# Two rotary tables move to the other queue's ring, behind the first slab, and an 8 KB transfer is put in front

## The chip, the cores and the metric

The kernel runs on one core of a Trainium2 chip. The metric is device time of one execution in microseconds (us), the median of three runs for the kernel before. Smaller is better.

## The reference

A rotary embedding: each head's two halves are rotated by tables that depend on the position alone. `x` is 16 x 512 x 1024 in float32, 16 heads of 64, so `half_dim` is 32; `cos` and `sin` are 512 x 32.

```python
x = x.reshape(batch, seq, num_heads, head_dim)
x1, x2 = x[..., :half_dim], x[..., half_dim:]
cos = cos[None, :, None, :]
sin = sin[None, :, None, :]
rotated = np.concatenate([x1 * cos - x2 * sin,
                          x1 * sin + x2 * cos], axis=-1)
```

## The kernel before, in words

The input is cut into 8 slabs of two batches, 4 MB each. A slab stands in SBUF as 128 partitions x 8192 float32: a partition has 8 consecutive rows of 1024, so one DMA of a slab is 128 descriptors of 32 KB. There are 6 slab buffers. A slab is worked on in place and stored from the same buffer.

Two queues issue DMAs. SyncE issues all loads of slabs (`load`, line 61): slabs 0 to 5 at the start, slabs 6 and 7 when the stores of slabs 0 and 1 have freed their buffers. ScalarE issues all stores (line 147), between its own casts, and in the kernel before also the two tables (`load_tables`, line 77). Each issuing engine feeds a ring of its own; the same 16 DMA engines serve both rings.

The tables take a way of their own. `cos` and `sin` are read as 16 rows of 4 KB each (`TR = 16`) into every eighth partition of the tile `raw`, which VectorE has set to zero before (line 69); the first table DMA waits for that memset. GpSimd builds 0/1 and -1 selection matrices in `pick` (lines 89 and 93), waits for both tables and casts `raw` to bf16 (`raw_b`, line 99). Then 16 matmuls (line 104) spread the 16 rows over the 128 partitions, and VectorE copies the result from PSUM into `tab` (line 110), the table that every later multiply reads. So no multiply can start before the tables have landed.

After that the slabs go through a pipeline of passes, half a slab each for the first and the last two slabs, a whole one for the others. ScalarE casts a pass to bf16 (line 129), one pass ahead; VectorE multiplies twice by `tab` (line 139) and adds (line 142); ScalarE casts back to float32 (line 145) and, with the last pass of a slab, issues its store.

The order of issue is written out by hand; each engine runs its instructions in program order, and the framework puts in the semaphores.

Of the kernel before, what the change touches and what calls it, by code (L numbers as in the profile page):

```python
# [2 lines left out]

# [4 lines left out]


@with_exitstack  # L10
def kernel(
    ctx: ExitStack,
    tc: tile.TileContext,
    x: bass.AP,
    cos: bass.AP,
    sin: bass.AP,
    num_heads: int,
    out: bass.AP,
):
    nc = tc.nc  # L20
    P = nc.NUM_PARTITIONS

    batch, seq, dim = x.shape
    nh = num_heads
    hd = dim // nh
    half = hd // 2
    bf16 = mybir.dt.bfloat16
    f32 = mybir.dt.float32

    nb = 2  # L30
    slots = 6
    nslabs = batch // nb
    rpp = nb * seq // P
    W = rpp * dim
    SP = seq // rpp
    TW = rpp * half

    out_flat = out.rearrange("b s h d -> b s (h d)")

    singles = ctx.enter_context(tc.tile_pool(name="singles", bufs=1))  # L40
    slabs = ctx.enter_context(tc.tile_pool(name="slabs", bufs=slots))
    psum = ctx.enter_context(tc.tile_pool(
        name="psum", bufs=1, space=bass.MemoryType.PSUM))


    def dram(t, s, a=0, n=W):
        return bass.AP(tensor=t.tensor, offset=t.offset + s * nb * seq * dim + a,
                       ap=[[W, P], [1, n]])


    def view(t, offset, *dims):
        return dataclasses.replace(t, offset=t.offset + offset,
                                   ap=[t.ap[0], *[list(d) for d in dims]])


    slab = {}


    def load(s):
        slab[s] = slabs.tile([P, W], f32, tag="slab", name="slab")  # L60
        nc.sync.dma_start(out=slab[s], in_=dram(x, s))  # L61

    TR = 16
    TQ = seq // TR // rpp
    TC = seq * half // TR
    raw = singles.tile([P, TC], f32, tag="raw")
    nc.vector.memset(raw, 0.0)  # L69


    def load_tables(queue):
        for i, src in enumerate((cos, sin)):
            to = dataclasses.replace(
                raw, offset=raw.offset + 4 * i * raw.ap[0][0],
                ap=[[P // TR * raw.ap[0][0], TR], [1, TC]])
            queue.dma_start(out=to, in_=bass.AP(  # L77
                tensor=src.tensor, offset=src.offset, ap=[[TC, TR], [1, TC]]))


    load(0)
    load_tables(nc.scalar)
    for s in range(1, slots):
        load(s)

    pick = singles.tile([P, 3 * TQ * P], bf16, tag="pick")
    nc.gpsimd.memset(pick, 0.0)  # L89
    for g in range(3):  # L90
        for j in range(TQ):
            part = view(pick, (g * TQ + j) * P + j, (SP, P // SP), (TQ, TR))
            nc.gpsimd.affine_select(  # L93
                out=part, in_=part, compare_op=mybir.AluOpType.not_equal,
                fill=-1.0 if g == 2 else 1.0, base=-4 if g else 0,
                pattern=[[0, P // SP], [-(P // TR), TR]], channel_multiplier=1)

    raw_b = singles.tile([P, TC], bf16, tag="raw_b")
    nc.gpsimd.tensor_copy(out=raw_b, in_=raw)  # L99

    acc = psum.tile([P, 2 * rpp * hd], f32, tag="acc")
    for g, at in ((0, 0), (0, half), (1, rpp * hd), (2, rpp * hd + half)):
        for j in range(TQ):
            nc.tensor.matmul(  # L104
                view(acc, at, (hd, rpp), (1, half)),
                view(pick, (g * TQ + j) * P, (1, P)),
                view(raw_b, j * TW, (half, rpp), (1, half)),
                start=j == 0, stop=j == TQ - 1)
    tab = singles.tile([P, 2 * rpp * hd], bf16, tag="tab")
    nc.vector.tensor_copy(out=tab, in_=acc)  # L110

    passes = []
    for s in range(nslabs):
        n = rpp if 1 <= s < nslabs - 2 else rpp // 2
        passes += [(s, r, n) for r in range(0, rpp, n)]


    def halves(u):
        s, r, n = u
        t = slab[s].bitcast(bf16)
        return [view(t, (2 * r + i * n) * dim, (1, n * dim)) for i in range(2)]


    def cast(u):
        s, r, n = u
        nc.scalar.copy(out=halves(u)[0], in_=view(slab[s], r * dim, (1, n * dim)))  # L129


    cast(passes[0])
    for i, u in enumerate(passes):
        s, r, n = u
        if i + 1 < len(passes):
            cast(passes[i + 1])
        lo, up = halves(u)
        for t, a in ((up, 0), (lo, rpp * hd)):
            nc.vector.tensor_mul(  # L139
                out=t, in0=lo,  # L140
                in1=view(tab, a + r * hd, (hd, n), (0, nh), (1, hd)))
        nc.vector.tensor_add(  # L142
            out=up, in0=up, in1=view(lo, half, (hd, n * nh), (-half, 2), (1, half)))

        nc.scalar.copy(out=view(slab[s], r * dim, (1, n * dim)), in_=up)  # L145
        if r + n == rpp:
            nc.scalar.dma_start(out=dram(out_flat, s), in_=slab[s])
            if s + slots < nslabs:
                load(s + slots)


# [1 line left out]
_INS = ['x', 'cos', 'sin', 'num_heads']  # L153
_OUTS = [((16, 512, 16, 64), 'float32')]

_NUMBERS = {'num_heads': 16}


# [26 lines left out]
```

## Time and profile before

| | |
|---|---|
| Median of 3 runs | 162.03 us (161.91 to 162.1) |
| The profiled execution | 161.88 us, its span 160.1 us |
| Busy: VectorE, ScalarE | 109.3 us (68%), 113.3 us (71%) |
| Busy: GpSimd, TensorE | 4.7 us (3%), 3.6 us (2%) |
| Bytes read and written | 33.69 MB and 33.55 MB, 420 GB/s over the span |
| The two DMA queues kept the 16 engines busy for | 49.3% and 48.8% of the span |
| Tables: issue to landing | `cos` 8.0 us, `sin` 10.1 us |

The profile is of one execution; its span runs from the first instruction to the last, and 1.78 us of the execution lie around it. A row of the timeline gives start and length in us, then engine, line and operation; in brackets stands how long the engine was idle before and what released it. The DMA share of a window is the mean busy share of the 16 DMA engines, with a packet counted where it starts, so that in short windows it can be over 1.

### The profile page before, as it was taken

Reading aid. Unit: us, or ns where it says so; the run is one execution under the profiler, and the core shown is the slowest. Engines: PE = TensorE matmul, PEld = TensorE weight load, DVE = VectorE, ACT = ScalarE, POOL = GpSimd, SP = SyncE. Lnnn points to the kernel's source line nnn. Section 1 sums busy time; section 2 is a strip of 40 time slices with the busy share of each in tenths; the row PEclk is TensorE's granted clock in tenths of the full one; section 3 lists DMA queues with packets and bytes.
Section 4 is the critical chain, followed back from the end, with each engine's and each line's share of the span. In section 5 each row is a group of like instructions: output and inputs, shape, how many; then the busy total and the mean of one; then the engine's idle time right before and its main releaser. Section 6 shows DMA issues by size and latency. Waiting matters only on the chain.

```text
span 160.1 us, 200 instructions
## 1 busy us (share of the span) xinstructions
PE 3.6 (2%) x16; PEld 2.3 (1%) x16; DVE 109.3 (68%) x35; ACT 113.3 (71%) x23; POOL 4.7 (3%) x18
## 2 busy tenths in 40 slices
PE   0005300000000000000000000000000000000000
PEld 0003100000000000000000000000000000000000
DVE  2000699999999989998996299939569499910000
ACT  2105939999979999999909995199995999280000
POOL 8002000000000000000000000000000000000000
DMA  7999999999999999999999999999999999999994
GB/s 246 426 385 418 393 442 475 393 418 483 409 393 483 434 393 442 475 393 409 499 401 393 508 409 393 483 434 393 434 483 393 393 516 401 393 508 409 393 475 180
DMA packets 2368, 67.24 MB, mean 420 GB/s; under 512 B 288, under 2 KB 288, under 8 KB 320
## 3 DMA queue, kind: packets, MB, share of 16 engines
q1 hardware_dynamic: 1152, 33.55, 49.3%
q10 hardware_dynamic: 1216, 33.69, 48.8%
HBM read 33.69 MB, written 33.55 MB: 420 GB/s over the span
## 4 chain that ended last, share of the span: by engine, by line
DMA 50%; DVE 21%; ACT 8%; issue 7%; PE 2%; POOLq 1%; ACTq 0%; DVEq 0%; SPq 0%
DMA slab<-in_x_dram 26%; DMA out_dram<-slab 17%; DVE slab L139 14%; DMA raw<-in_sin_dram 6%; DVE slab L142 6%; ACT slab L145 5%; ACT slab L129 3%; PE acc L104 2%; DVE tab L110 1%; POOLq L180 1%; DVE raw L69 1%; ACTq L77 0%; POOLq L99 0%; DVEq L139 0%; SPq L61 0%
## 5 line engine op out<-in xcount | busy, mean ns | idle before, releaser
L139 DVE TENSOR_TENSOR slab<-slab,tab 128x4096 bf16<-128x4096 bf16 (+1 forms) x22 | 71.6, 3260 | 14.3 <-ACT slab L129 13.8
L129 ACT CAST slab<-slab 128x4096 bf16<-128x4096 f32 (+1 forms) x11 | 56.6, 5153 | 23.1 <-DMA slab<-in_x_dram 23.1
L145 ACT CAST slab<-slab 128x4096 f32<-128x4096 bf16 (+1 forms) x11 | 56.6, 5153 | 4.6 <-DVE slab L142 4.6
L142 DVE TENSOR_TENSOR slab<-slab 128x4096 bf16<-128x4096 bf16 (+1 forms) x11 | 35.9, 3260 | 0.3
L110 DVE CAST tab<-acc 128x1024 bf16<-128x1024 f32 x1 | 1.2, 1225 | 15.5 <-PE acc L104 15.5
L104 PE MATMUL acc<-raw_b,pick 128*128 128x256 bf16 x16 | 3.6, 415 | 13.9 <-POOL raw_b L99 13.9
L129 ACT ACT_TABLE_LOAD x1 | 1.3, 1283 | 3.2 <-issue 3.2
L104 PEld LDWEIGHTS <-pick 128*128 128x128 bf16 x16 | 2.3, 142 | 14.7 <-issue 11.3
L93 POOL TENSOR_SCALAR_AFFINE_SELECT pick<-pick 128x32 bf16<-128x32 bf16 x12 | 2.1, 257 | 0.1
L69 DVE MEMSET raw<- 128x1024 f32 x1 | 0.9, 912 | 1.0 <-PEq L166 1.0
L89 POOL MEMSET pick<- 128x1536 bf16 x1 | 1.4, 1377 | 0.3 <-POOLq L166 0.3
L99 POOL CAST raw_b<-raw 128x1024 bf16<-128x1024 f32 x1 | 1.0, 1036 | 8.5 <-DMA raw<-in_sin_dram 8.5
L166 POOL MEMSET const-float32-0.0<- 128x1 f32 x1 | 0.1, 98 | 0.2 <-issue 0.2
L166 POOL MEMSET const-bfloat16-1.0<- 128x1 bf16 x1 | 0.1, 102 | 0.0
L166 POOL MEMSET const-uint8-127<- 128x1 uint8 x1 | 0.1, 102 | 0.0
L166 POOL MEMSET const-float32-1.0<- 128x1 f32 x1 | 0.1, 98 | 0.0
## 6 DMA issues: line engine op xcount, KB each, us to landing
slab<-in_x_dram SPq DMA_DIRECT2D x8, 4096.0 KB, 42.4
out_dram<-slab ACTq DMA_DIRECT2D x8, 4096.0 KB, 26.1
raw<-in_cos_dram ACTq DMA_DIRECT2D x1, 64.0 KB, 8.0
raw<-in_sin_dram ACTq DMA_DIRECT2D x1, 64.0 KB, 10.1
```

The lines of the kernel that those rows point to most:

```text
L69: nc.vector.memset(raw, 0.0)
L89: nc.gpsimd.memset(pick, 0.0)
L93: nc.gpsimd.affine_select(out=part, in_=part, compare_op=mybir.AluOpType.not_equal, fill=-1.0 if g == 2 else 1.0, base=-4 if g else 0, pat ...
L99: nc.gpsimd.tensor_copy(out=raw_b, in_=raw)
L104: nc.tensor.matmul(view(acc, at, (hd, rpp), (1, half)), view(pick, (g * TQ + j) * P, (1, P)), view(raw_b, j * TW, (half, rpp), (1, half)), ...
L110: nc.vector.tensor_copy(out=tab, in_=acc)
L129: nc.scalar.copy(out=halves(u)[0], in_=view(slab[s], r * dim, (1, n * dim)))
L139: nc.vector.tensor_mul(out=t, in0=lo, in1=view(tab, a + r * hd, (hd, n), (0, nh), (1, hd)))
L142: nc.vector.tensor_add(out=up, in0=up, in1=view(lo, half, (hd, n * nh), (-half, 2), (1, half)))
L145: nc.scalar.copy(out=view(slab[s], r * dim, (1, n * dim)), in_=up)
L166: nc = _bacc.Bacc("TRN2", target_bir_lowering=False, num_devices=1)
L180: with _tile.TileContext(nc) as tc:
```

## The change

The tables' two DMAs are issued by SyncE, after slab 0 and before slab 1. ScalarE issues a new DMA as its first instruction: 16 rows of 128 floats of `cos`, 16 descriptors of 512 B, into a tile `first` that nothing reads. It waits for nothing.

```diff
+    first = singles.tile([TR, P], f32, tag="first")
+    nc.scalar.dma_start(out=first, in_=bass.AP(
+        tensor=cos.tensor, offset=cos.offset, ap=[[TC, TR], [1, P]]))
     load(0)
-    load_tables(nc.scalar)
+    load_tables(nc.sync)
     for s in range(1, slots):
         load(s)
```

All lines behind it have numbers higher by four in the kernel after.

## The prediction

> **What bounds the kernel now.** I read the page first: the 40 slices of the span, then the DMA totals and the chain that ended last.
>
> ```profile
> DVE  2000699999999989998996299939569499910000
> ACT  2105939999979999999909995199995999280000
> DMA  7999999999999999999999999999999999999994
> HBM read 33.69 MB, written 33.55 MB: 420 GB/s over the span
> DMA 50%; DVE 21%; ACT 8%; issue 7%; PE 2%; POOLq 1%; ACTq 0%; DVEq 0%; SPq 0%
> ```
>
> The DMA row is 9 from the second slice to the next to last; VectorE and ScalarE have holes and are idle in the last 16 us. The transfers bound the kernel. Only three things can then move the end: when the byte stream starts, how many bytes it has, and how much engine time a byte takes. The next view is the timeline around the start.
>
> ```profile
> 1.96 0.56 ACTq L77 DMA_DIRECT2D raw<-in_cos_dram  x1
> 2.55 0.61 ACTq L77 DMA_DIRECT2D raw<-in_sin_dram  x1
> 12.77 1.04 POOL L99 CAST raw_b<-raw 128x1024 bf16<-128x1024 f32 x1 [8.52 <-DMA raw<-in_sin_dram]
> 13.86 7.11 ACT L129 CAST slab<-slab 128x4096 bf16<-128x4096 f32 x2 [9.38 <-DMA slab<-in_x_dram]
> 17.47 1.23 DVE L110 CAST tab<-acc 128x1024 bf16<-128x1024 f32 x1 [15.54 <-PE acc L104]
> 18.79 6.82 DVE L139 TENSOR_TENSOR slab<-slab,tab 128x4096 bf16<-128x4096 bf16 x3
> 23.57 7.02 ACT L129 CAST slab<-slab 128x8192 bf16<-128x8192 f32 x1 [2.60 <-DMA slab<-in_x_dram]
> ```
>
> The casts released by arriving slabs date the arrivals: slab 0 at 13.86, slab 1 at 23.57. A slab of 4096 KB alone in the queues takes 9.71 us, 432 GB/s. The last store is issued at 144.27 and lands 14.8 us later (the shortest landing of line 147), at 159.07. From 13.86 to there are 145.2 us for 15 more slabs' worth of loads and stores, and 15 x 9.71 is 145.7: behind slab 0 the stream has no gap. So the change is decided in the first 13.86 us. How dear the bytes are there is in the windows (core 0: window, its length, busy time of PE, PEld, DVE, ACT, POOL with counts, clock, DMA share, GB/s; a packet counts where it starts):
>
> ```profile
> 1.50:3.00 1.50, 0.00 (x0) 0.10 (x1) 0.43 (x1) 0.00 (x0) 1.43 (x6) 1.00 1.26 350
> 3.00:5.50 2.50, 0.00 (x0) 0.00 (x0) 0.00 (x0) 1.28 (x1) 1.25 (x8) 1.00 0.98 419
> 5.50:7.80 2.30, 0.00 (x0) 0.00 (x0) 0.00 (x0) 0.00 (x0) 0.00 (x0) 1.00 1.10 442
> 7.80:10.90 3.10, 0.00 (x0) 0.00 (x0) 0.00 (x0) 0.00 (x0) 0.00 (x0) 1.00 0.98 381
> 10.90:13.00 2.10, 0.00 (x0) 0.00 (x0) 0.00 (x0) 0.00 (x0) 0.23 (x1) 1.00 0.73 312
> 37.00:61.00 24.00, 0.00 (x0) 0.00 (x0) 23.14 (x6) 22.89 (x5) 0.00 (x0) 1.00 1.01 437
> ```
>
> Share divided by GB/s is engine time for a byte. The clean rate is 1.01/437, and 10.90 to 13.00 is near it. Between 5.50 and 10.90, when the tables' packets pass, it is dearer. At the clean rate 442 GB/s would be a share of 1.02, so 0.08 x 2.3 = 0.18 us is lost; 381 would be 0.88, so 0.10 x 3.1 = 0.31 us. Together 0.49 us for each engine, on top of the tables' own 128 KB (0.30 us at 432 GB/s). I call this the mixing surcharge. The first wave, 1.50 to 3.00, is one 32 KB packet for each of 16 engines (350 GB/s x 1.5 us / 16): 1.26 x 1.5 = 1.89 us instead of 1.01 x 32.8 KB x 16 / 437 GB/s = 1.21 us. So 0.68 us is lost to the cold start.
>
> **The change, part by part.**
>
> *Tables leave ScalarE's ring.* The same two DMAs, 32 descriptors of 4 KB, now stand behind slab 0 in one ring; their 0.30 us of bytes stay. What becomes of the 0.49 us? In before the small items (two table packets and two completion writes on each engine) came from a second ring between slab 0's 32 KB packets. The trace has no 4 KB packet behind a 32 KB one in the same ring, so I bound it: at the dear end nothing is saved, at the other all 0.49. The nearest row is a completion write inside SyncE's ring, at the seam of slabs 0 and 1: the window 13.00 to 23.00 has a share of 1.06 at 455 GB/s, 1.052 at the clean rate, a loss of some 0.08 us over 10 us that holds a seam. I take 0.43 us saved, nearer to that row, because the loss is not seen where one ring works alone.
>
> The Trainium skill speaks against this step ("DMA: Bandwidth & Descriptors", section "Issuing engines are not separate DMA queues"): DMAs from any issuing engine end on the same 16 DMA engines and interleave, and issuing from another one only saves issue time. By that rule alone the surcharge would follow the tables into the other ring, and this step would be worth 0 instead of 0.43 us. The page gives no price for small packets of one ring between large ones of another; the windows above do.
>
> *SyncE's queue.* The table DMAs wait for the memset of `raw` (0.91 us from 1.01, done at 1.92). They stand now in front of the issues of slabs 1 to 5. Slab 1's issue, until now right behind slab 0's, goes to about 1.96 + 0.56 + 0.61 = 3.1 us, and slabs 2 to 4 follow at some 0.4 us each (line 61 issues: median 395 ns), by 5 us. In the program's order slab 4's issue also waits for the semaphore that the short DMA uses, slab 5's still for slab 0's. All is covered by slab 0 and the tables, which keep the engines busy until about 13 us; without that cover it would cost 2 us. On ScalarE the table DMAs and their wait go; its table load can start earlier, off the path, because its first cast waits for slab 0.
>
> *The tables' landing.* Slab 0 lands earlier by 0.30 + 0.43, at 13.1. The tables come right after, at about 13.4 instead of 12.62, when sin landed. The chain behind them keeps its lengths: POOL's cast 1.04, 16 matmuls 3.57, VectorE's cast 1.23. So VectorE's first multiply moves from 18.79 to about 19.6. What is late next? ScalarE and VectorE are 0.8 us later until ScalarE meets its wait for slab 5 at 84 us, where it now idles 3.85 us (the same timeline): the delay ends there. Store 0 is later by as much, but loads fill the engines meanwhile (loads 4 and 5 are still in the ring, load 5 until 84 us). At the end, 159.07 - 9.71 = 149.4 is when the engines reach the last store, 5.1 us after its issue; an issue takes 1.0 us to the first packet (0.73 to 1.7), so some 4 us of cover remain. Cost: 0. It costs only what exceeds 3.9 us.
>
> *The short DMA.* 8 KB is 0.02 us at 432 GB/s. Each engine has two more small items from ScalarE's ring, a 512 B packet and a completion write. The trace has no such packet ahead of the stream. Upper bound: the four small items of before cost 0.49, so two cost 0.25. Lower bound: part of the first wave's 0.68 us cold loss can pass under the short packet, because on ScalarE nothing stands in front of it, as on SyncE nothing stands in front of slab 0 (first issue at 0.73), and it brings 512 B to an engine against 32 KB; but nothing shows it arriving much before slab 0's own packets, so I allow a gain of at most 0.3. I take +0.01 over the bytes, 0.03 in all, since it comes where the engines wait anyway.
>
> *Two issues at once.* The short DMA and slab 0 are issued at the same time. SyncE's issues last 328 to 616 ns, the long ones beside ScalarE's table issues (563 and 609). If the two get in each other's way, slab 0's descriptors come later by 0 to 616 - 328 = 0.29 us, or by the whole of ScalarE's issue, 0.61, if that goes first. I take 0: slab 0's packets now start 1.0 us after their issue, which is longer than the issue, and the cold loss is there in any case.
>
> Sum: -0.43 + 0.03 + 0 = -0.40 us. The profiled execution took 161.88 (span 160.1 and 1.78 around it), so 161.48 for it; it lies 0.15 below the median of the runs, 162.03, so 161.63, stated as 161.6.
>
> **The rivals.**
>
> Slower: the short DMA holds up the stream. Slab 0's first packets can't start before ScalarE's small descriptors are out, or wait behind them for a memory round trip. Price 0.61 us (ScalarE's longest issue) + 0.02. It decides if half of the surcharge or more stays (0.25 saved): 162.03 + 0.63 - 0.25 = 162.4. In general the kernel is slower once the delay exceeds the saving by 0.32 us. For it: the stretched issues of both engines around 2 us. Against it: 16 descriptors are few, and SyncE may win the race. Chance 0.27.
>
> No difference: the surcharge belongs to 4 KB packets in whichever ring they stand, and the short DMA is lost in the cold start: 162.03 + 0.03 = 162.06. For it: all engines in those windows lose alike, and a part of the loss could be the tables' writes into other partitions than the engine's own. Against it: the clean windows on either side. Or the saving and a start delay of 0.3 to 0.6 cancel; that gives the same time. Chance 0.22.
>
> The change doesn't do what it says: the tables' later landing delays the stores so much that the loads run dry. It would need over 3.9 us and the sum has 0.8; chance 0.01, with the slower.
>
> **How the numbers follow.** Faster, 0.50: saving 0.43 with a start effect between -0.3 and +0.1 gives 161.3 to 161.7. A difference of 0.2%, 0.32 us, is about what a measurement of this kernel can tell from no change. For 8 in 10 the range runs from the fast case with the whole cold gain (161.63 - 0.06 - 0.3 = 161.3, and 0.1 for the runs' own spread: 161.2) over no difference to the slower rival with its price, 162.4, and 0.1 more: 162.5. The likeliest case's own range is 161.2 to 161.7. Faster 0.50, same 0.22, slower 0.28.
>
> **What would show it.** Right: in windows of 2 to 3 us between 3 and 13 us, share over GB/s stays near 1.01/437; slab 0's cast starts near 13.1 instead of 13.86, POOL's cast near 13.5, VectorE's first multiply near 19.6, slab 1's cast near 23.2; the last store's landing moves by as much as slab 1's arrival, no more. Wrong: slab 0's cast at 13.5 or later, and first-wave packets that start after 2 us; or a dear window just behind slab 0, where the tables pass; or DMA slices under 9 in the middle of the span.

## The result, and the profile after

| | before | after |
|---|---|---|
| Median | 162.06 us (161.91 to 162.25, 6 executions) | 170.18 us (167.55 to 173.15, 6 executions) |
| The profiled execution | 161.88 us, span 160.1 us | 172.36 us, span 170.6 us |
| Ratio after to before | | 1.0348, interval 1.0331 to 1.0366 |

The changed kernel is slower. Its six executions lie in two groups, three at 167.55 to 167.99 and three at 172.36 to 173.15; the ratio is that of the lower group (the ratios below are likewise of a run's faster executions), and the profile is of an execution in the upper; the lower group has no profile, so that it loses in the same way is not shown.

First the row of the DMA engines and the totals, of the page of the kernel after, as read before:

```profile
DVE  2000599999999989989960799339387499800000
ACT  3008849899699999999039980199993999160000
DMA  6999999999899999999999999999999999858930
HBM read 33.69 MB, written 33.55 MB: 394 GB/s over the span
```

The slices are 4.3 us long. Up to 145 us the engines are as busy as before, but for one slice at 8; the last six slices (8 5 8 9 3 0) have holes. Over the whole span the rate is 394 GB/s instead of 420. So up to 145 us no ring ran dry: the same bytes took longer to move. The holes behind that come from an earlier delay, shown below. Then the start, in the timeline of the kernel after:

```profile
13.54 7.11 ACT L133 CAST slab<-slab 128x4096 bf16<-128x4096 f32 x2 [11.09 <-DMA slab<-in_x_dram]
14.09 1.04 POOL L103 CAST raw_b<-raw 128x1024 bf16<-128x1024 f32 x1 [9.82 <-DMA raw<-in_sin_dram]
20.11 8.90 DVE L143 TENSOR_TENSOR slab<-slab,tab 128x4096 bf16<-128x4096 bf16 x4
23.55 7.02 ACT L133 CAST slab<-slab 128x8192 bf16<-128x8192 f32 x1 [2.90 <-DMA slab<-in_x_dram]
28.93 4.49 DVE L146 TENSOR_TENSOR slab<-slab 128x4096 bf16<-128x4096 bf16 x2
31.31 7.11 ACT L149 CAST slab<-slab 128x4096 f32<-128x4096 bf16 x2 [0.74 <-DVE slab L146]
38.45 0.36 ACTq L151 DMA_DIRECT2D out_dram<-slab  x1
```

Slab 1 arrives at 23.55, as before (23.57). Up to here nothing is lost. But VectorE now makes four multiplies and then two additions. Before, the three multiplies at 18.79 were followed by an addition, a multiply and an addition, and store 0 went out at 37.63:

```profile
25.53 2.28 DVE L142 TENSOR_TENSOR slab<-slab 128x4096 bf16<-128x4096 bf16 x1
27.73 2.29 DVE L139 TENSOR_TENSOR slab<-slab,tab 128x4096 bf16<-128x4096 bf16 x1
30.05 2.29 DVE L142 TENSOR_TENSOR slab<-slab 128x4096 bf16<-128x4096 bf16 x1
37.63 0.35 ACTq L147 DMA_DIRECT2D out_dram<-slab  x1
```

The text of both kernels has two multiplies and an addition for each pass; neither runs them so, because the framework's scheduler settles the order when the program is built. The first addition ends so late that ScalarE waits 0.74 us for it, and store 0 is issued at 38.45 instead of 37.63.

The loss is later. The windows of the kernel before, and then those of the kernel after (columns as above: the last two are DMA share and GB/s):

```profile
37.00:43.50 6.50, 0.00 (x0) 0.00 (x0) 6.46 (x2) 6.50 (x2) 0.00 (x0) 1.00 1.05 449
43.50:51.00 7.50, 0.00 (x0) 0.00 (x0) 7.47 (x3) 6.39 (x2) 0.00 (x0) 1.00 1.03 446
51.00:80.00 29.00, 0.00 (x0) 0.00 (x0) 27.61 (x7) 29.00 (x5) 0.00 (x0) 1.00 1.00 433
144.00:157.50 13.50, 0.00 (x0) 0.00 (x0) 0.00 (x0) 0.24 (x1) 0.00 (x0) 1.00 1.01 437
```

```profile
37.00:43.50 6.50, 0.00 (x0) 0.00 (x0) 6.43 (x3) 6.50 (x2) 0.00 (x0) 0.50 1.01 408
43.50:51.00 7.50, 0.00 (x0) 0.00 (x0) 7.50 (x2) 6.14 (x2) 0.00 (x0) 0.50 1.03 446
51.00:80.00 29.00, 0.00 (x0) 0.00 (x0) 27.58 (x8) 29.00 (x5) 0.00 (x0) 0.50 1.00 410
144.00:157.50 13.50, 0.00 (x0) 0.00 (x0) 4.43 (x2) 4.68 (x2) 0.00 (x0) 0.50 0.78 337
```

Between 37 and 43.5 us, when the stores begin, the kernel after is dearer (408 GB/s against 449): some load packets are long there. From 43.5 to 51 us the two are alike. From 51 us on the kernel after has full engines and 5% less throughput (410 to 433 GB/s): packets take longer. What follows is a delay handed on. The load of slab 6, which waits for store 0, is issued at 65.15 instead of 61.17; that of slab 7 at 88.05 instead of 80.47; the last store at 152.18 instead of 144.27, 7.9 us later. Before that issue most engines have nothing left to move: the share is 0.33 between 148 and 152.2 us. The last store lands 17.3 us after its issue instead of 14.8, because a few engines are still behind. These 7.9 and 2.5 us are the span's 10.5 but for 0.1.

**Which packets are slow.** The trace also holds every DMA packet with its start, its length and its queue. On one engine a packet starts some 4 ns before the one before it ends, so the packets can be strung together into 16 engines. Read so, an engine that has both rings to serve mostly alternates single 32 KB packets, a load and a store; from 44 us on, nine in ten take about 1213 ns. In the kernel after, between 44 and 58.5 us, 15 store packets take more than 1260 ns, and they are all on the same five engines, three on each:

```
engine   loads before    last loads before the     slow stores (start us, ns)
         its first store  first store, ns
three of 11 others:
         32               1218                     none
         32               1276                     none
         32               1762                     none
the five:
         33               1409, 1856               51.17 1788   54.16 1873   57.24 1369
         33               1628, 1856               51.25 1819   54.27 1872   57.35 1406
         33               1645, 1772               51.24 1781   54.23 1878   57.31 1368
         33               1658, 1831               51.39 1794   54.39 1856   57.45 1500
         33               2159, 1213               51.91 1714   54.83 1858   57.90 1467
```

A slab is 8 packets for an engine, so 32 loads are slabs 0 to 3. The five had begun slab 4 before their first store, the other eleven had not. In the kernel before nine engines had 32 loads and seven had 31, and no store packet is slow.

These few engines carry the loss. From 51 to 119 us, 118 store packets of the kernel after take more than 1260 ns, together 43.8 us above 1213; in the kernel before there are none. If all of it is on the five, that is 8.8 us each. Five engines end their loads at 127.5 us or later and the other eleven at 120; at the end, five finish between 167.4 and 169.2 us and eleven at 162.8 or 162.9. Before, all 16 finish between 158.3 and 158.7. A slab has landed only when its last engine has, so slab 7 lands 7.9 us later and holds up the last store for all engines. Why some engines are slow is what the experiments are about.

### The profile page after: what moved, and what is told of

Read it like the earlier page. It is cut to its first block, busy times and chain, and to the rows that moved or that the text cites. A ratio compares the mean times of both kernels' runs of the same rounds, so it can differ in the third digit from the quotient of the medians.

```text
span 170.6 us, 201 instructions
## 1 busy us (share of the span) xinstructions
PE 3.6 (2%) x16; PEld 2.3 (1%) x16; DVE 109.1 (64%) x35; ACT 113.4 (67%) x23; POOL 4.7 (3%) x18
## 4 chain that ended last, share of the span: by engine, by line
DMA 52%; DVE 20%; issue 8%; ACT 7%; PE 2%; POOLq 1%; SPq 0%; DVEq 0%; ACTq 0%
DMA slab<-in_x_dram 25%; DMA out_dram<-slab 20%; DVE slab L143 13%; DMA raw<-in_sin_dram 7%; DVE slab L146 5%; ACT slab L149 4%; ACT slab L133 2%; PE acc L108 2%; DVE tab L114 1%; POOLq L184 1%; DVE raw L69 1%; SPq L77 0%; POOLq L103 0%; DVEq L143 0%; SPq L61 0%
```

## The experiments

**Half the change at a time, the tile, and a late table.** e1 has the tables on SyncE and no short DMA; e2 the short DMA, with the tables where they were; e3 only the tile that the short DMA fills; e4 the kernel before with the table copied twice.

```diff
 e1 (against after)
-    first = singles.tile([TR, P], f32, tag="first")
-    nc.scalar.dma_start(out=first, ...)
 e2 (against before)
+    first = singles.tile([TR, P], f32, tag="first")
+    nc.scalar.dma_start(out=first, ...)
     load(0)
     load_tables(nc.scalar)
 e3 (against before)
+    first = singles.tile([TR, P], f32, tag="first")
...
+    nc.gpsimd.memset(first, 0.0)
 e4 (against before)
     nc.vector.tensor_copy(out=tab, in_=acc)
+    nc.vector.tensor_copy(out=tab, in_=acc)
```

> Half of the change: the tables go behind slab 0 in SyncE's ring, and there is no short DMA. Theory A (phase: the tables' later landing moves store 0's issue by some 0.8 us, and the moment at which ScalarE's ring wakes, within a 1.21 us packet, decides whether the 16 engines alternate loads and stores in two opposite groups or all in step): store 0 is issued near 38.4 us as in the kernel after, so the time is 166 to 174 us. Theory B (the short DMA spoils ScalarE's ring, or the 512 B tile shifts the slabs): without it 161.5 to 162.3 us.

> The other half: the short DMA ahead of all else, the tables behind it in ScalarE's ring as before. Theory A: the tables land as before, store 0 is issued at 37.6 us as before or within 0.1 us of it, so 161.9 to 162.4 us. Theory B: the short DMA is the cause, so 166 to 174 us.

> The kernel before with the tile of the short DMA allocated, which shifts the slabs in SBUF by 512 B a partition, but no DMA into it; GpSimd clears it in idle time. Theory A: 161.9 to 162.3 us. Theory C (the place of the slabs in SBUF decides how the engines get in each other's way): 166 to 174 us.

> The kernel before, all DMAs as they were, with VectorE's copy of the table made twice: its first multiply moves from 18.8 to about 20.0 us, as in the kernel after, and store 0's issue from 37.6 to about 38.4 us. Theory A: 166 to 174 us, with all engines changing between loads and stores together in the stretch from 42 to 60 us. Theories B and C, and any that blames a ring or the short DMA: 161.9 to 162.5 us, since 1.2 us is less than the slack of 3.9.

e1: 171.74 us (169.51 to 174.94), ratio 1.0485 (1.0448 to 1.0521). e2: 162.19 us, ratio 1.0016 (1.0004 to 1.0028). e3: 162.00 us, ratio 0.9995 (0.9985 to 1.0004). e4: 161.98 us, ratio 0.9993 (0.9984 to 1.0002). The moved tables alone bring the loss; the short DMA costs about 0.2% and theories B and C fall. e4 seems to speak against theory A too, but its store did not move as meant: VectorE began its multiplies at 20.10 us, as in the kernel after, and kept its old order, so that ScalarE still had its second pass in time and issued store 0 at 37.88 instead of 37.63, hardly more than slab 1's own arrival moved (23.81 instead of 23.57). So a late table is not by itself a late store.

**Table packets in the rings, and two attempts at a late store.** e5 keeps the real tables in ScalarE's ring and puts copies that nothing reads behind slab 0 in SyncE's; e6 is e1 with such copies in ScalarE's ring. e7 and e8 add a copy on ScalarE ahead of store 0.

```diff
 e5 (against before)
     load_tables(nc.scalar)
+    spare = singles.tile([P, TC], f32, tag="spare")
+    load_tables(nc.sync, spare)
 e6 (against e1)
     load_tables(nc.sync)
+    spare = singles.tile([P, TC], f32, tag="spare")
+    load_tables(nc.scalar, spare)
 e7, e8 (against before; 700 and 300 elements)
         if r + n == rpp:
+            if s == 0:
+                nc.scalar.copy(out=scr, in_=view(slab[0], 0, (1, 700)))
```

> The kernel before, with its tables in ScalarE's ring, and a second copy of both tables, which nothing reads, behind slab 0 in SyncE's ring, as the changed kernel has them (128 KB more, 0.3 us). The compute and store 0 keep their times. Theory A (the later stores are the cause): 162.1 to 162.8 us. Theory D (table packets in SyncE's ring, which shift its later descriptors, are the cause): 166 to 174 us. Theory G (ScalarE's ring without table packets is the cause): 162.1 to 162.8 us.

> The changed kernel without its short DMA, with a second copy of both tables, which nothing reads, in ScalarE's ring at the start, as the kernel before has them. The tables that count still land behind slab 0 and store 0 is late. Theories A and D: 166 to 174 us. Theory G: 162 to 163 us.

> The kernel before with a copy of 700 elements on ScalarE ahead of store 0's issue, so that this goes out some 0.8 us later, near 38.4 us as in the kernel after; all rings and VectorE's order as before. Theory A: 166 to 174 us. Theories D and G: 161.9 to 162.5 us, the 0.8 us being inside the slack.

> As the last one with a copy of 300 elements, so that store 0 goes out some 0.4 us later, near 38.0 us. Theory A: slow (166 to 174 us) or not, depending on which side of a packet's 1.21 us the store falls; theories D and G: 161.9 to 162.4 us.

e5: 164.15 us (163.48 to 164.24). It changed more than was meant: the scheduler put ScalarE's cast of slab 1 behind its first cast back, and store 0 went to 41.95 us. It tells only that table packets in SyncE's ring with a store far later do not give 167 us or more. e6: median 165.15, ten executions from 162.4 to 173.43, so both outcomes in one program; theory G, that ScalarE's ring lacks packets, falls. e7: 162.01, e8: 162.06 us, ratios 0.9987 and 0.9992; they say nothing, because store 0 waits for ScalarE's cast back and not for the copy, and was issued at 37.85 and 37.75.

**A store that is truly late.** Here ScalarE copies a piece of slab 0 onto itself, and the store must wait for that. The edit is the same in all, with the number of elements changed.

```diff
 e9, e10 (against before; 1300 and 1650 elements), e11, e12 (against after; 1300 and 2650)
         if r + n == rpp:
+            if s == 0:
+                again = view(slab[0], 0, (1, 1300))
+                nc.scalar.copy(out=again, in_=again)
```

> The kernel before, with ScalarE copying 1300 elements of slab 0 onto themselves ahead of its store, which must wait for that: store 0 goes out some 1.2 us later, near 38.8 us. All rings, the tables and VectorE as before. Theory H (the cause is the packet at which the stores wake ScalarE's ring: where some engines have begun slab 4 and others have not, the ones ahead are slowed): 165 to 175 us here or in the next one. Theory D (the tables in SyncE's ring are the cause): 161.9 to 162.5 us.

> The same with 1650 elements, store 0 some 1.5 us later, near 39.1 us. Theory H: 165 to 175 us here or in the one before, as the mix of engines at the boundary has it. Theory D: 161.9 to 162.5 us.

> The changed kernel with store 0 some 1.2 us later, near 39.7 us, when all engines are past the boundary of slabs 3 and 4. Theory H: the slow transfers go, 161.5 to 163 us. Theory D: 166 to 175 us as in the kernel after.

> The changed kernel with store 0 some 2.4 us later, near 40.8 us, a whole packet or more behind the boundary. Theory H: 161.5 to 163 us. Theory D: 166 to 175 us.

e9: 162.29 us (1.0016, 1.0006 to 1.0027), store 0 at 39.01. e10: 162.26 us (1.0016, 1.0004 to 1.0027), at 39.38. e11: 162.46 us (161.96 to 163.64; ratio 1.0033, 1.0012 to 1.0055), at 39.26. e12: 163.95 us (1.0119, 1.0102 to 1.0136), at 40.78. e11 is the turning point: the changed kernel, with its tables in SyncE's ring, is rid of its loss of 5 us and more when its first store goes out 0.8 us *later*. Its slab 1, its store 0 and the window in which the kernel after was at 410 GB/s:

```profile
23.56 7.02 ACT L133 CAST slab<-slab 128x8192 bf16<-128x8192 f32 x1 [2.90 <-DMA slab<-in_x_dram]
39.26 0.36 ACTq L154 DMA_DIRECT2D out_dram<-slab  x1
51.00:80.00 29.00, 0.00 (x0) 0.00 (x0) 27.62 (x7) 29.00 (x5) 0.00 (x0) 0.50 1.00 429
```

So theory D is not enough, and no slack or wait can explain the loss: delay takes it away. In the packets of e11 no engine has 32 loads before its first store; they have 33 or 34. e12's 1.9 us are not in its stores, none of which is over 1340 ns. They are in its loads: from 44 us on 79 of them take 1.26 to 2.02 us, 28.8 us above 1213 or 1.8 us for each of 16 engines, where the kernel before has none. So the stores' moment can make loads slow as well; what decides which was not tested.

**The same moment, from the other side.** A common scale is the time, in the profiled execution of each run, from slab 1's arrival (the cast of 8192 elements that it releases) to store 0's issue: 14.06 us in the kernel before, e2, e3 and e4; 14.80 in e6, 14.84 in e1 and 14.90 in the kernel after; 15.24 in e9, 15.53 in e10 and 15.71 in e11. e13, e14 and later e17 put the kernel before into the gap, with 400, 680 and 895 elements in the edit above. e15 is e1 with 1300. e16 shifts addresses:

```diff
 e16 (against after)
-        nc.sync.dma_start(out=slab[s], in_=dram(x, s))
+        nc.sync.dma_start(out=slab[s], in_=dram(x, s, -2 * W if s >= 4 else 0))
```

> The kernel before, with ScalarE copying 400 elements of slab 0 onto themselves ahead of its store: store 0 some 0.6 us later, near 38.2 us, where it is in the kernel with the tables alone on SyncE. Theory H (the moment of the first store against the load packets, whatever the rings hold): 165 to 175 us here or in the next. Theory D2 (table packets in SyncE's ring are needed too): 161.9 to 162.5 us.

> The same with 680 elements: store 0 near 38.45 us, where it is in the kernel after. Theory H: 165 to 175 us here or in the one before. Theory D2: 161.9 to 162.5 us.

> The tables alone on SyncE, without the short DMA, with 1300 elements copied ahead of store 0, which goes from 38.2 to near 39.4 us. Theories H and D2 both: the slow transfers go as they did in the kernel after with the same delay, 161.5 to 163.5 us; were it still at 168 us or more, the moment of the first store would not be what matters.

> The kernel after; slabs 4 to 7 are read from 64 KB (two partitions' rows) further ahead in x, so those slabs hold other rows than they should. Bytes, descriptors and timing are the same. Theory of addresses (a store's packets are slow while loads of other engines read HBM at a matching place): the time changes clearly, to 161.5 to 164 us. Theory of engines (only the order of packets within and between the engines counts): 166 to 175 us as in the kernel after.

e13: 161.89 us (ratio 0.9989, 0.9979 to 0.9998), at 14.49 on the scale. e14: 161.92 us (0.9992, 0.9982 to 1.0002), at 14.72 and not at 14.9 as meant; nine executions at 161.73 to 162.15 and one at 167.98. e15: 162.55 us (1.0037, 1.0018 to 1.0055), at 16.09; delay takes the loss away in e1 too. e16: 171.68 us (165.78 to 173.41), at 14.95: with the later loads' addresses 64 KB off the loss stays, so for this shift the theory of addresses falls. Its packets show the pattern again: five engines have 33 loads before their first store, and those five alone have slow stores up to 58.5 us, 1319 to 1912 ns.

**The last two.** e17 puts the kernel before at 14.9; e18 gives the kernel after its old order on VectorE.

```diff
 e18 (against after)
-            nc.vector.tensor_mul(
+            mul = nc.vector.tensor_mul(
...
+        if i == 0:
+            first_add = add
+        if i == 1:
+            tc.add_manual_dep(mul.ins, first_add.ins.name, ...)
```

> The kernel before, with ScalarE copying 895 elements of slab 0 onto themselves ahead of its store: store 0 at 14.9 us after slab 1's arrival (near 38.5 us), the rings and the tables as before. Theory H (that moment alone decides): most executions at 164 to 175 us. Theory D2 (the tables in SyncE's ring are needed too): 161.9 to 162.5 us with at most one slow execution in ten.

> The kernel after in full, with one dependency that makes VectorE add the first pass before it multiplies the second pass a second time, which is its order in the kernel before. Store 0 goes back from 38.45 to some 37.8 us, 14.1 to 14.3 us after slab 1's arrival. Theory H: 161.4 to 162.2 us, the change being harmless by itself and worth what the prediction said of the start, 0 to 0.5 us. Theory D2: 165 us or more, since the tables are still in SyncE's ring and land late.

e17: 170.3 us, executions at 163.3, 167.62, 170.12, 170.47, 172.8 and 173.36. It is the kernel before, with its tables in ScalarE's ring and no short DMA; its one edit takes 0.93 us on ScalarE. Its timeline, and its windows as shown for the other two:

```profile
23.87 7.02 ACT L129 CAST slab<-slab 128x8192 bf16<-128x8192 f32 x1 [2.59 <-DMA slab<-in_x_dram]
37.81 0.93 ACT L149 COPY slab<-slab 128x895 f32<-128x895 f32 x1
38.77 0.35 ACTq L150 DMA_DIRECT2D out_dram<-slab  x1
```

```profile
43.50:51.00 7.50, 0.00 (x0) 0.00 (x0) 7.26 (x3) 7.50 (x2) 0.00 (x0) 1.00 1.06 450
51.00:80.00 29.00, 0.00 (x0) 0.00 (x0) 27.87 (x7) 29.00 (x5) 0.00 (x0) 1.00 1.00 417
```

The share is 1.00 and the rate falls to 417 GB/s from 51 us on, the signature of the kernel after. In its packets four engines have 33 loads before their first store and twelve have 32; up to 58.5 us the slow stores (1418 to 1855 ns) are on those four alone. VectorE keeps the order of the kernel before. Against it e14's timeline and window; it differs by 215 elements, and all 16 engines are at 32 in its profile:

```profile
37.48 0.75 ACT L149 COPY slab<-slab 128x680 f32<-128x680 f32 x1
38.26 0.35 ACTq L150 DMA_DIRECT2D out_dram<-slab  x1
```

```profile
51.00:80.00 29.00, 0.00 (x0) 0.00 (x0) 27.61 (x7) 29.00 (x5) 0.00 (x0) 1.00 1.00 434
```

So the first store's moment is enough. With every DMA as it was, the kernel is at 162 us when that moment is 0.2 or 0.4 us earlier (e14 but for one execution, e13) or 0.3 us later (e9), and at 167 or more in five of six executions here. It is not the whole of it. e18 brings store 0 back to 37.72, 14.06 on the scale, and was expected at 161.4 to 162.2 us; of thirteen executions seven are at 162.02 to 162.47 and six at 168.1 to 173.74. Its store 0 and window are of the profiled execution, at 172.94:

```profile
37.72 0.36 ACTq L156 DMA_DIRECT2D out_dram<-slab  x1
51.00:80.00 29.00, 0.00 (x0) 0.00 (x0) 27.58 (x8) 29.00 (x5) 0.00 (x0) 1.00 1.00 420
```

In its packets two engines have 31 loads before the first store, eleven 32 and three 33, and the stores up to 58.5 us are slow on those three alone (1336 to 1901 ns). The tables in SyncE's ring therefore matter beside the moment. In what way was not tested. The loads in flight when the stores begin are longer in e18 on most engines (up to 1947 ns, against 1213 to 1353 in e14). The engines may also be less closely in step: the 31st loads of the 16 engines start within 0.62 to 0.84 us of each other in the eight profiles with the real tables in SyncE's ring, and within 0.43 to 0.69 in eleven of the twelve others; but in e10, which is at 162 us, it is 0.89.

## Why the prediction was wrong, step by step

**The step that failed** is "Cost: 0" for the tables' later landing, with its reason that "loads fill the engines meanwhile" and that the delay "costs only what exceeds 3.9 us". The price of a packet was taken as fixed once the stream runs, and it depends on how loads and stores are interleaved on the engines: on a few of the 16 engines the stores' packets became longer, together by 43.8 us, and a slab waits for its last engine. e17 shows that a copy of 0.93 us, far within the slack, costs 5.6 to 11.3 us in five of six executions with nothing else changed; e11 shows that 0.8 us more takes the cost away. That store 0 was late by the 0.8 us that had been said (37.63 to 38.45) is luck: VectorE's first multiply came at 20.11 and not at 19.6, and the store's delay came from another cause, its order of work (below). A slack measured on the clock does not cover a change of phase.

**What bounds the kernel**: right, the transfers. Wrong was the conclusion that "the change is decided in the first 13.86 us". It was drawn from a stream without gaps; the stream after has none up to 145 us either, and is 5% slower from 51 us on.

**The mixing surcharge** went where it was seen: from 5.50 to 10.90 us the kernel after is at the clean rate. But it came back in part behind slab 0, where the tables now pass, a place that the prediction had named as the sign of its error:

```profile
5.50:7.80 2.30, 0.00 (x0) 0.00 (x0) 0.00 (x0) 0.00 (x0) 0.00 (x0) 1.00 1.06 456
7.80:10.90 3.10, 0.00 (x0) 0.00 (x0) 0.00 (x0) 0.00 (x0) 0.00 (x0) 1.00 0.88 381
10.90:13.00 2.10, 0.00 (x0) 0.00 (x0) 0.00 (x0) 0.00 (x0) 0.00 (x0) 1.00 1.24 496
```

1.06/456 and 0.88/381 are 1.01/437 again. In the last row 496 GB/s would be 1.146 at the clean rate: 0.094 x 2.1 = 0.20 us. Of the 0.43 us that the prediction took as saved, slab 1's arrival shows 0.02 in this pair; slab 0's cast came at 13.54 and not at 13.1, slab 1's at 23.55 and not at 23.2. Other pairs show more: slab 1 arrives 0.34 us earlier in e1 than in e3, 0.21 in e11 than in e9, 0.21 in e18 than in e17 and 0.10 in e16 than in e14. So this term was too large, but not worth nothing. The rule of the Trainium skill ("DMA: Bandwidth & Descriptors", "Issuing engines are not separate DMA queues"), by which issuing from another engine saves issue time alone, would have made it 0; these rows lie between the two. Which ring the small transfer is in moved the rest of the kernel by 5 us and more (e1).

**The order on VectorE** differs between the two programs: four multiplies and two additions against three, one, one, one. The prediction moved the chain in time and kept its order. That put the store's delay on the wrong cause: e4, with an equally late first multiply and the old order, has its store 0 at 14.07 us on the scale and e18, with the tables landing late, at 14.06, as in the kernel before; with the new order it is 14.90.

**The short DMA**: 0.03 us was said, with 0.27 as its bound from above. e2 measures 0.16% (0.04% to 0.28%), 0.06 to 0.45 us: near the upper bound rather than the value taken. At slab 1's arrival only 0.05 us of it is seen (23.74 against 23.69 in e3).

**The rivals.** The slower one had the right sign and the wrong mechanism: the stream's start was not held up, since slab 1 arrives when it did. The one given 0.01, late stores that let the loads run dry, was nearest in that it began with late stores; but the loads never ran dry, and the only holes, just before and after the last store's issue, follow from the slow engines.

## What to carry to other kernels

When the DMA engines are busy from end to end, ask not only whether an edit opens a gap but whether it changes which load packet each engine is at when the other ring begins; divide share by GB/s in windows along the whole span, for a rate can fall without a hole. Look also at when each engine ends, for a few late engines hold up every slab. A kernel in that state can owe its time to a lucky phase: before trusting a small edit, or a small gain, shift the first store by half a packet both ways and take several executions. Compare the instruction order of both programs engine by engine before pricing a delay, since the scheduler may answer a later input with another order.

No run beats the kernel before by as much as 0.2%: the lowest are e7 at 0.9987 (0.9974 to 1.0) and e13, with its first store 0.4 us later on the scale, at 0.9989 (0.9979 to 0.9998).

## What the runs showed of the hardware that was not expected

- Store packets of 32 KB that take more than 1.26 us (1.71 to 1.91 for an engine's fourth and fifth) instead of 1.21, from the fourth one of the engine on, on just those engines that began slab 4 before their first store while most others did not. This holds in the five profiles of executions above 170 us (after, e1, e16, e17, e18), with 5, 2, 5, 4 and 3 such engines of 16; as many engines finish late there, 4 us or more behind the rest. Splits at another packet (31 and 32 loads in the kernel before, 33 and 34 in e11 and e15, 34 and 35 in e5 and e12) have no store over 1.43 us. The split alone is not sufficient: in e6's profile (162.94 us) two engines are one load ahead and none is slow, and in e9's, where eleven are ahead and five are not, the slow ones up to 58.5 us stay at 1.28 to 1.42 us. In e6 and e9 the last loads of the engines ahead took 1.21 to 1.25 us; in the five profiles at least one of them took 1.39 to 2.56. Why these stores are slow, and why from the fourth on, stays open; a shift of the loads' addresses by 64 KB does not change it.
- The times on the scale from slab 1's arrival to store 0: 14.06 and 14.49 us always under 163 with the tables in ScalarE's ring, 14.72 one execution of ten at 168, 14.90 five of six at 167 or more, 15.24 and 15.53 back at 162. With the tables in SyncE's ring: 14.06 (e18) and 14.80 (e6, with copies in ScalarE's ring) both outcomes, 14.84 and 14.90 always 167 or more (e1, the kernel after), 14.95 three of four at 170 or more (e16), 15.71 and 16.09 at 162 to 163.7.
- The granted clock of TensorE, 1.0 in some executions and 0.56 to 0.57 in others, has nothing to do with it: the kernel after took 167.62 us at 1.0 and 167.55 at 0.567.
